# Transposing the blocks of a short convolution one pipeline tick later, with one input buffer turned into a working tile

## The chip, the core and the metric

The kernel runs on one core of a Trainium2 chip. The metric is device time in microseconds (us) of one execution, on a median of several runs. The core's engines work side by side, each through an instruction queue of its own: PE (TensorE, matrix products and transposes, with PEld for the loading of its stationary operand), DVE (VectorE), ACT (ScalarE), POOL (GpSimd) and SP (SyncE, which here issues the DMA transfers). [...]

## The reference, cut to what matters

The model is a two-layer backbone over 2048 latent tokens and 256 context tokens of width 1024. Layer 0 holds two groups of heads side by side, a gated DeltaNet with four heads of 128 (group A) and grouped-query attention (group B); layer 1 is a Conformer convolution. Every layer ends in an output projection and a gated residual. The change lies in the first step of group A. From the normalized, modulated input h and the weight w_in it computes 1536 channels (512 each of q, k and v), convolves each channel along the tokens with five taps, applies SiLU, and brings q and k of each head to unit length:

```python
def gdn_prep(qkv, a, b, conv_w, a_log, dt_bias):
    u = jax.nn.silu(depthwise_conv(qkv, conv_w))         # qkv = (h @ w_in)[:, :1536], 5 taps over tokens
    q, k, v = split_cols(u, [512, 512, 512])
    q = l2_normalize(heads(q, A_DK)) * (A_DK ** -0.5)    # a * rsqrt(sum(a * a) + NORM_EPS), per token and head
    k = l2_normalize(heads(k, A_DK))
    v = heads(v, A_DV)
    ...
```

The context tokens of k and v (not of q) go through the same step apart from the latent ones.

## The kernel before

All products are made of float32 values split into a high and a low part: `mm3` (L135 to L139) issues three matmuls for each slice of 128 of the contraction, high by high (L137), and the two cross terms (L138 and L139). With eight slices, one tile of products is 24 matmuls. `split` (L141) makes the two parts of a weight, the high one on ACT (L145), the low one mostly on POOL (L148).

Layer 0's input half runs as three stages: one that normalizes and transposes the tokens and projects the attention's values, then stage A (pool `stA`, L340 to L357), then stage B, which projects what is left. A long mixed stage follows (scan of the DeltaNet and attention), then the output projection and layer 1.

Stage A works in 56 blocks. A channel tile `ct` is one head of q (0 to 3), k (4 to 7) or v (8 to 11), and each has four blocks of 512 latent tokens; for k and v there is a fifth, of the 256 context tokens. `a_item` (L450) is the work of one block, cut in steps by `yield`:

- The 24 matmuls into a PSUM tile `ps_a` (pool `mm`, four tiles); the copy by ACT to the tile `ub` in SBUF (L459, five buffers); small copies by DVE that carry two tokens over from and to the neighbour block (L464, L465). With the second block of a channel tile the next tile's weights are loaded and split.
- An empty tick, then the taps: two multiplications by ACT into `acc` and `p1` (L474, L475), their sum by POOL (L476), three more taps by DVE (L478), and SiLU by ACT in place (L480). For q the result goes to memory here.
- One tick later the block is turned by PE with up to four transposes of 128 by 128 into `psT` (L488; pool `tp`, four PSUM tiles). For v, ACT copies it to `tok` (L492) and it is stored. For q and k, ACT squares it (L496), DVE sums the squares and scales them (L498, L500), and POOL raises to the power of -1/2 (L151). For q this is all; for k, DVE multiplies by the result into `tok` (L507) and it is stored.
- For k there is a further tick: four transposes back, `psB` (L513), a copy by ACT to `bt` (L515), and a store (L516).

`acc`, `p1`, `sq`, `bt` and a tile `ada_part` of another step share the tag `wk`, with five buffers in all. That step, `ada_late` (L1160), computes six pieces of the modulation of later stages: weights by DMA (L1170), multiply-adds by DVE (L1176, L1178), and small products by PE (`ps_adat`, L1183). It advances after the first and the fourth block of each channel tile.

Two things set the order on the engines. `pipe` starts one block per tick and then takes every block in flight one step on, newest first, so that the tick of a `yield` sets which block's matmuls are written ahead of which block's taps and transposes. What is written so is then ordered for each engine by a list scheduler, which takes the order of writing as the priority, holds an instruction back until it expects its operands and its buffer to be ready, and puts a later one in its place. A buffer of a tag comes from a pool of free ones, so that the number of buffers also takes part in the order. The order is fixed when the kernel is built; on the chip each engine follows its own.

Of the kernel before, what the change touches and what calls it, by code (L numbers as in the profile page):

```python
# [8 lines left out]
F32 = mybir.dt.float32  # L9
# [8 lines left out]
P = 128  # L18
# [90 lines left out]
class Build:  # L109
# [178 lines left out]
    def layer0_in(self):  # L288
        tc, nc = self.tc, self.nc
        with ExitStack() as es:  # L290
# [49 lines left out]
            with tc.tile_pool(name="stA", bufs=2, reuse_waits="tile") as st:  # L340
                self.ada1 = [self.kp.tile([P, 8], F32, name=f"ada1{x}") for x in "AB"]
                self.gcol = [self.kp.tile([P, 8], F32, name=f"gcol{x}") for x in range(2)]
                late = self.ada_late([(1, 2), (1, 0), (1, 3), (1, 1), (0, 4), (0, 5)],
                                     lambda: st.tile([P, 512], F32, tag="wk", name="ada_part", bufs=5))
                items = []
                cols = [ct * P for ct in range(12)]
                for ct in range(12):
                    blocks = [(0, 512), (1, 512), (2, 512), (3, 512)]
                    if ct >= 4:
                        blocks.append((4, TC))  # L350
                    shared = {}
                    for b, n in blocks:
                        items.append(self.a_item(ct, b, n, shared, st, cols[ct + 1] if ct < 11 else None))
                        if b in LATE_B:
                            items.append(late)
                self.pipe(items)
                self.pipe([late])  # L357
# [92 lines left out]
    def a_item(self, ct, b, n, shared, st, nxt):  # L450
        nc = self.nc
        kind, h = "qkv"[ct // 4], ct % 4
        whi, wlo = self.w0(ct * P, P)
        if b == 1 and nxt is not None:
            self.w0(nxt, P)
        ps = self.mm.tile([P, 512], F32, tag="mm", name="ps_a")
        self.mm3(ps[:, :n], [(whi[k], wlo[k], self.hhi[b][:, k, :], self.hlo[b][:, k, :]) for k in range(KT)])
        ub = st.tile([P, 516], F32, tag="ub", name="ub", bufs=5)
        nc.scalar.copy(ub[:, 2:2 + n], ps[:, :n])  # L459
        if b in (0, 4):  # L460
            nc.vector.memset(ub[:, 0:2], 0.0)
        else:
            prev = shared[b - 1]
            nc.vector.tensor_copy(ub[:, 0:2], prev[:, 512:514])  # L464
            nc.vector.tensor_copy(prev[:, 514:516], ub[:, 2:4])  # L465
        if b >= 3:
            nc.vector.memset(ub[:, 2 + n:4 + n], 0.0)
        shared[b] = ub
        yield
        yield  # L470
        w = [self.col("scw", ct * 5 + j) for j in range(5)]
        acc = st.tile([P, 512], F32, tag="wk", name="acc", bufs=5)
        p1 = st.tile([P, 512], F32, tag="wk", name="p1", bufs=5)
        nc.scalar.mul(acc[:, :n], ub[:, 0:n], w[0])  # L474
        nc.scalar.mul(p1[:, :n], ub[:, 1:1 + n], w[1])  # L475
        nc.gpsimd.tensor_tensor(out=acc[:, :n], in0=acc[:, :n], in1=p1[:, :n], op=ALU.add)  # L476
        for j in range(2, 5):
            nc.vector.scalar_tensor_tensor(out=acc[:, :n], in0=ub[:, j:j + n], scalar=w[j], in1=acc[:, :n],  # L478
                                           op0=ALU.mult, op1=ALU.add)
        nc.scalar.activation(acc[:, :n], acc[:, :n], AF.Silu)  # L480
        m = n // P
        tt0 = b * 4
        if kind == "q":
            nc.sync.dma_start(self.d_qT[h, :, tt0 * P:tt0 * P + n], acc[:, :n])
        yield
        psT = self.tp.tile([P, 4, P], F32, tag="tp", name="psT")
        for a in range(m):
            nc.tensor.transpose(psT[:, a, :], acc[:, a * P:(a + 1) * P], self.ident)  # L488
        if kind != "q":
            tok = st.tile([P, 4, P], F32, tag="tok", name="tok", bufs=3)  # L490
        if kind == "v":
            nc.scalar.copy(tok[:, :m, :], psT[:, :m, :])  # L492
            nc.sync.dma_start(self.d_v[tt0:tt0 + m, :, h * P:(h + 1) * P].rearrange("a p c -> p a c"), tok[:, :m, :])
            return
        sq = st.tile([P, 4, P], F32, tag="wk", name="sq", bufs=5)
        nc.scalar.activation(sq[:, :m, :], psT[:, :m, :], AF.Square)  # L496
        ss = st.tile([P, 4], F32, tag="ss", name="ssA")
        nc.vector.reduce_sum(ss[:, :m], sq[:, :m, :], axis=AX.X)  # L498
        f = 128.0 if kind == "q" else 1.0
        nc.vector.tensor_scalar(out=ss[:, :m], in0=ss[:, :m], scalar1=EPS, scalar2=f, op0=ALU.add, op1=ALU.mult)  # L500
        if kind == "q":

            self.rsqrt(self.rq[:, tt0:tt0 + m, h], ss[:, :m], m)
            return
        rn = st.tile([P, 4], F32, tag="rn", name="rn")
        self.rsqrt(rn[:, :m], ss[:, :m], m)
        nc.vector.tensor_tensor(out=tok[:, :m, :], in0=psT[:, :m, :],  # L507
                                in1=rn[:, :m].unsqueeze(2).to_broadcast([P, m, P]), op=ALU.mult)
        nc.sync.dma_start(self.d_k[tt0:tt0 + m, :, h * P:(h + 1) * P].rearrange("a p c -> p a c"), tok[:, :m, :])
        yield  # L510
        psB = self.tp.tile([P, 512], F32, tag="tp", name="psB")
        for a in range(m):
            nc.tensor.transpose(psB[:, a * P:(a + 1) * P], tok[:, a, :], self.ident)  # L513
        bt = st.tile([P, 512], F32, tag="wk", name="bt", bufs=5)
        nc.scalar.copy(bt[:, :n], psB[:, :n])  # L515
        nc.sync.dma_start(self.d_kT[h, :, tt0 * P:tt0 * P + n], bt[:, :n])  # L516

# [1029 lines left out]
```

## Time and profile before

| | |
|---|---|
| median of 3 runs | 2611.97 us (2608.75 to 2613.16) |
| profiled execution | 2612.17 us, span of its trace 2610.4 us, mean granted PE clock 0.99 |
| busy PE | 2518.3 us, 96% of the span |
| busy DVE, ACT, POOL | 1979.2 us (76%), 1466.5 us (56%), 1401.5 us (54%) |
| stage A on PE | from 112.28 us (first `ps_a`) to about 458 us (last `psT`) |
| memory traffic | 323.24 MB, mean 124 GB/s |

How to read it: the span is the time from the first to the last instruction of the trace, and lies 1.8 us below the time of the same execution. Busy times are sums over instructions; in a row of the timeline stand the start, the time, the engine, the line of the kernel and the operation with its output and inputs, and in brackets how long the engine sat idle before it and what ended that idle time. A row of the windows gives the busy time and the instructions of PE, PEld, DVE, ACT and POOL in a stretch, the granted PE clock as a share of full speed, the DMA share and GB/s. A row of the waits gives who waited for what, the total, the number of times and the longest.

### The profile page before, as it was taken

What the parts mean: (1) busy time and instruction counts of PE and PEld (TensorE: products, weight loads), DVE (VectorE), ACT (ScalarE), POOL (GpSimd) and SP (SyncE); (2) the same over time, 40 slices, a digit from 0 to 9 for tenths busy, and PEclk for the clock granted to TensorE, in tenths of its full rate; (3) what the DMA queues carried; (4) which work ended last, traced back from release to release, by engine and by line L of the source; (5) the groups of instructions that cost most, each with busy time, mean ns of one, the idle gap of its engine ahead of it and who ended that gap; (6) DMA issues with size and microseconds to landing.
All of it is one profiled execution on the core that took longest, in us unless ns stands there. A gap on an engine that the chain in (4) does not pass through costs nothing.

```text
span 2610.4 us, 43411 instructions
## 1 busy us (share of the span) xinstructions
PE 2518.3 (96%) x15072; PEld 2203.3 (84%) x15072; DVE 1979.2 (76%) x4118; ACT 1466.5 (56%) x3101; POOL 1401.5 (54%) x1189
## 2 busy tenths in 40 slices
PE   7999999999999799999999999999999999999998
PEld 5988878998888698999989998888888888888877
DVE  7566677676764787788777787746389999998875
ACT  7444456223776565656666666534266767666443
POOL 3344344566446473553354423012169999899775
PEclk9999999999999899999999999999999999999999
DMA  8133334334565755645564433134411211115643
GB/s 316 50 113 108 111 115 126 107 109 140 163 193 175 202 126 134 146 124 139 147 164 131 132 102 114 40 106 129 153 49 42 67 54 65 53 57 176 205 160 109
DMA packets 410747, 323.24 MB, mean 124 GB/s; under 512 B 131232, under 2 KB 339616, under 8 KB 410528
## 3 DMA queue, kind: packets, MB, share of 16 engines
q1 hardware_dynamic: 410528, 320.47, 41.1%
q8 instruction: 120, 1.97, 0.3%
q14 instruction: 99, 0.81, 0.1%
HBM read 216.05 MB, written 104.33 MB: 123 GB/s over the span
## 4 chain that ended last, share of the span: by engine, by line
PE 53%; DVE 7%; ACT 2%; issue 2%; DMA 2%; POOL 1%; SPq 0%; POOLq 0%; DVEq 0%; ACTq 0%
PE pt L1114 4%; PE ps_out L137 3%; PE ps_out L139 3%; PE ps_out L138 3%; PE pg L139 2%; PE pa L137 2%; PE pg L138 2%; PE pg L137 2%; PE pa L138 2%; PE pa L139 2%; PE pz L137 2%; PE pz L139 2%; PE pz L138 2%; PE po L1144 2%; PE po L1145 2%; PE po L1148 2%
## 5 line engine op out<-in xcount | busy, mean ns | idle before, releaser
L1406 DVE SCALAR_TENSOR_TENSOR pc<-u,hw,pc 128x1024 f32<-128x1024 f32 x320 | 390.0, 1281 | 5.2 <-ACT pc L1404 3.9
L1414 POOL TENSOR_TENSOR ac<-ac,pr 128x512 f32<-128x512 f32 x288 | 379.5, 1341 | 18.0 <-ACT pr L1413 4.4
L1413 ACT ACTIVATE pr<-u,hw 128x512 f32<-128x512 f32 x288 | 204.9, 721 | 91.3 <-POOL ac L1414 89.8
L1118 ACT CAST phi<-pt 128x512 fp32r<-128x512 f32 x288 | 164.5, 585 | 144.8 <-PE pt L1114 136.7
L137 PE MATMUL ps_b<-w_hi,hhi 128*128 128x256 f32 (+1 forms) x800 | 231.3, 291 | 8.8 <-DVE xn L572 6.8
L1119 DVE TENSOR_TENSOR plo<-pt,phi 128x512 fp32r<-128x512 f32 x288 | 195.6, 687 | 49.9 <-ACT phi L1118 46.7
L138 PE MATMUL ps_b<-w_lo,hhi 128*128 128x256 f32 (+1 forms) x800 | 227.6, 286 | 0.9 <-DVE w_lo L148 0.8
L139 PE MATMUL ps_b<-w_hi,hlo 128*128 128x256 f32 (+1 forms) x800 | 225.0, 287 | 0.6 <-POOL hlo L148 0.6
L1073 DVE TENSOR_SCALAR_CACHE_REDUCE S<-ps_s 128x512 f32<-128x512 f32 (+1 forms) x320 | 198.8, 631 | 16.1 <-PE ps_s L139 11.0
L1082 ACT ACTIVATE S<-S,m 128x1024 f32<-128x1024 f32 (+1 forms) x192 | 177.8, 929 | 49.0 <-DVE m L1079 48.5
L137 PE MATMUL ps_out<-wohi,yhi 128*128 128x512 f32 x512 | 201.9, 394 | 0.2 <-DVE x L1250 0.2
L139 PE MATMUL ps_out<-wohi,ylo 128*128 128x512 f32 x512 | 200.6, 393 | 1.4 <-DVE ylo L148 1.4
L138 PE MATMUL ps_out<-wolo,yhi 128*128 128x512 f32 x512 | 200.8, 392 | 0.0
L1144 PE MATMUL po<-phi,vhi 128*128 128x256 f32 x576 | 164.8, 306 | 14.4 <-ACT phi L1118 14.3
L1114 PE MATMUL pt<-ident,S 128*128 128x128 f32 x1152 | 175.3, 274 | 2.8 <-DVE plo L1119 1.9
L137 PE MATMUL ps_a<-hhi,w_hi 128*128 128x512 f32 (+1 forms) x448 | 172.1, 384 | 0.0
L138 PE MATMUL ps_a<-hlo,w_hi 128*128 128x512 f32 (+1 forms) x448 | 171.9, 384 | 0.0
L139 PE MATMUL ps_a<-hhi,w_lo 128*128 128x512 f32 (+1 forms) x448 | 171.3, 382 | 0.0
L478 DVE SCALAR_TENSOR_TENSOR acc<-ub,cols,acc 128x512 f32<-128x512 f32 (+1 forms) x168 | 136.4, 820 | 39.8 <-POOL acc L476 35.9
L137 PEld LDWEIGHTS ps_b<-w_hi,hhi 128*128 128x128 f32 x800 | 152.5, 191 | 12.2 <-issue 6.0
L138 PEld LDWEIGHTS ps_b<-w_lo,hhi 128*128 128x128 f32 x800 | 152.8, 191 | 2.3 <-DVE w_lo L148 1.8
L1145 PE MATMUL po<-phi,vlo 128*128 128x256 f32 x576 | 153.6, 286 | 0.0
(327 smaller groups left out, 7667.1 us busy)
## 6 DMA issues: line engine op xcount, KB each, us to landing
raw_ada<-in_ada_w_dram SPq DMA_DIRECT2D x48, 512.0 KB, 3.9
x<-in_x_dram SPq DMA_DIRECT2D x32, 512.0 KB, 10.3
kq<-d_kT SPq DMA_DIRECT2D x54, 256.0 KB, 3.1
raw_w<-in_ev_w_in_dram SPq DMA_DIRECT2D x26, 512.0 KB, 3.7
kq<-d_qT SPq DMA_DIRECT2D x48, 256.0 KB, 4.1
raw_w<-in_od_w_in_dram SPq DMA_DIRECT2D x24, 512.0 KB, 3.8
d_nt<-ntA SPq DMA_DIRECT2D x36, 256.0 KB, 4.3
vt<-d_v SPq DMA_DIRECT2D x36, 256.0 KB, 2.6
```

What stands on the lines that cost most here:

```text
L137: self.nc.tensor.matmul(ps, lhsT=lh, rhs=rh, start=(a == 0), stop=False)
L138: self.nc.tensor.matmul(ps, lhsT=lh, rhs=rl, start=False, stop=False)
L139: self.nc.tensor.matmul(ps, lhsT=ll, rhs=rh, start=False, stop=(a == n - 1))
L1073: nc.vector.tensor_scalar(out=S[g][:, k0:k0 + w], in0=ps[:, :w], scalar1=1.0, scalar2=None, op0=ALU.mult, op1=ALU.max, accum_out=mx[:, b:b ...
L1082: nc.scalar.activation(S[g], S[g], AF.Exp, bias=m, scale=scale, accum_out=l[:, g:g + 1])
L1114: nc.tensor.transpose(pt[:, e, a * P:(a + 1) * P], S[a][k0 // 1024][:, k0 % 1024:k0 % 1024 + P], self.ident)
L1119: nc.vector.tensor_tensor(out=lo, in0=pt, in1=hi.bitcast(F32), op=ALU.subtract)
L1144: nc.tensor.matmul(po, lhsT=vhi[:, ks], rhs=hi[:, e, :], start=(k == 0), stop=False)
L1145: nc.tensor.matmul(po, lhsT=vlo[:, ks], rhs=hi[:, e, :], start=False, stop=False)
L1406: nc.vector.scalar_tensor_tensor(out=pc, in0=s(j), scalar=w(j), in1=pc, op0=ALU.mult, op1=ALU.add)
L1413: nc.scalar.mul(pr, s(j), w(j))
L1414: nc.gpsimd.tensor_tensor(out=ac, in0=ac, in1=pr, op=ALU.add)
```

## The change

A second `yield` stands ahead of the transposes, so all that follows SiLU (the transposes, and for v the copy and store, for q and k the squares, sums and powers, for k the scaled tile, its store and the whole last step) is written one tick later than before. The tag `wk` gets six buffers where it had five, and `ub` four where it had five. The instructions and their operands are the same, and their number on every engine; from line 486 on, the changed kernel's lines count one more.

```diff
-                                     lambda: st.tile([P, 512], F32, tag="wk", name="ada_part", bufs=5))
+                                     lambda: st.tile([P, 512], F32, tag="wk", name="ada_part", bufs=6))
...
-        ub = st.tile([P, 516], F32, tag="ub", name="ub", bufs=5)
+        ub = st.tile([P, 516], F32, tag="ub", name="ub", bufs=4)
...
-        acc = st.tile([P, 512], F32, tag="wk", name="acc", bufs=5)
-        p1 = st.tile([P, 512], F32, tag="wk", name="p1", bufs=5)
+        acc = st.tile([P, 512], F32, tag="wk", name="acc", bufs=6)
+        p1 = st.tile([P, 512], F32, tag="wk", name="p1", bufs=6)
...
         yield
+        yield
         psT = self.tp.tile([P, 4, P], F32, tag="tp", name="psT")
...
-        sq = st.tile([P, 4, P], F32, tag="wk", name="sq", bufs=5)
+        sq = st.tile([P, 4, P], F32, tag="wk", name="sq", bufs=6)
...
-        bt = st.tile([P, 512], F32, tag="wk", name="bt", bufs=5)
+        bt = st.tile([P, 512], F32, tag="wk", name="bt", bufs=6)
```

The scheduler then lays the engines' orders anew. On PE, before, around the transposes of the block number 32 (counted from 0, a block of k): `ps_a_3712` is the product of block 40 and `ps_a_3758` that of block 41.

```order
L139 MATMUL ps_a_3712<-hhi4_115,w_lo_3208 128x256
L137 MATMUL ps_a_3712<-hhi4_115,w_hi_3207 128x256
L138 MATMUL ps_a_3712<-hlo4_116,w_hi_3207 128x256
L139 MATMUL ps_a_3712<-hhi4_115,w_lo_3208 128x256
L488 MATMUL psT_3433<-ident_62,acc_3361 128x128 x4
L137 MATMUL ps_a_3758<-hhi0_110,w_hi_3531 128x512
L138 MATMUL ps_a_3758<-hlo0_111,w_hi_3531 128x512
```

So before, nine products have been made, counting from block 32's own, when block 32 is turned. On PE, after the change, the transposes of the same block, where `ps_a_3512` is the product of block 37:

```order
L139 MATMUL ps_a_3512<-hhi1_412,w_lo_3185 128x512
L137 MATMUL ps_a_3512<-hhi1_412,w_hi_3184 128x512
L138 MATMUL ps_a_3512<-hlo1_413,w_hi_3184 128x512
L489 MATMUL psT_3470<-ident_62,acc_3340 128x128 x4
L139 MATMUL ps_a_3512<-hhi1_412,w_lo_3185 128x512
L137 MATMUL ps_a_3512<-hhi1_412,w_hi_3184 128x512
```

They have moved up, into the midst of block 37's product, behind five whole products and a third of a sixth. Counted over the whole stage, the products that lie ahead of a block's transposes number, before, four at the start, more and more from block 16 on up to nine at blocks 32 to 37, and four again from block 49; after, five to six at all blocks up to 51. At the last four blocks both orders have four, three, two and one.

On ACT, before, at the copies and multiplications of the k tiles (`ub_2921` is block 27's, and the copies to `ub` since then are those of `ub_2982`, `ub_3041`, `ub_3105` and `ub_3166`):

```order
L459 COPY ub_3166<-ps_a_3141 128x512
L515 COPY bt_3013<-psB_3008 128x512
L474 ACTIVATE acc_3046<-ub_2921,cols_60 128x512
L475 ACTIVATE p1_3047<-ub_2921,cols_60 128x512
L496 ACTIVATE sq_3061<-psT_3055 128x512
L515 COPY bt_3073<-psB_3070 128x256
L474 ACTIVATE acc_3109<-ub_2982,cols_60 128x512
```

A block's multiplications stand behind the copies of the four blocks after it. On ACT, after, at the same copy, block 31's, which is now `ub_3143` (`ub_3020` is block 29's):

```order
L459 COPY ub_3143<-ps_a_3118 128x512
L480 ACTIVATE acc_3088<-acc_3088 128x512
L516 COPY bt_3115<-psB_3112 128x256
L474 ACTIVATE acc_3146<-ub_3020,cols_60 128x512
L475 ACTIVATE p1_3147<-ub_3020,cols_60 128x512
L497 ACTIVATE sq_3161<-psT_3155 128x512
L145 CAST w_hi_3508<-raw_w_3506 128x1024
```

Here a block's multiplications stand behind the copies of one or two blocks after it. Beyond stage A the scheduler's times have moved too. In stage B the order is as before. In a part of the mixed stage, which follows at some 890 to 1260 us, it isn't; on ACT, before, around the copies of a DeltaNet state (`sbC`, L847 and L848) between the casts of the attention's turned scores (`phi`, L1118):

```order
L1118 CAST phi<-pt 128x512
L919 ACTIVATE W<-psw 64x2x64 x2
L1118 CAST phi<-pt 128x512
L847 ACTIVATE sbC<-sbT 64x1024
L848 ACTIVATE sbC<-sbT 64x1024
L1118 CAST phi<-pt 128x512 x4
```

On ACT, after, at the same place:

```order
L920 ACTIVATE W<-psw 64x2x64 x4
L1119 CAST phi<-pt 128x512
L848 ACTIVATE sbC<-sbT 64x1024
L1119 CAST phi<-pt 128x512
L849 ACTIVATE sbC<-sbT 64x1024
L1119 CAST phi<-pt 128x512 x3
```

One cast has moved between the two copies. On SP, two loads of `ada_late`'s weights stand earlier than before, and the stores of k and v one block later.

## Prediction

> **What bounds the kernel now.** I read the page first, then the windows by stage, then PE's waits in stage A, then its timeline around them, and last the two orders. The page's head:
>
> ```profile
> PE 2518.3 (96%) x15072; PEld 2203.3 (84%) x15072; DVE 1979.2 (76%) x4118; ACT 1466.5 (56%) x3101; POOL 1401.5 (54%) x1189
> ```
>
> PE is busy for 96% of the span, and no other engine comes near it. So a change that leaves the instructions alone can win only what PE waits, or what it loses to a lower clock. The windows: the q part of stage A, its k and v part, the start of stage B, and the part of the mixed stage whose order changes.
>
> ```profile
> 112.00:206.00 94.00, 94.00 (x442) 77.92 (x441) 55.41 (x108) 44.23 (x72) 42.56 (x29) 1.00 0.33 104
> 206.00:458.00 252.00, 242.83 (x1294) 205.45 (x1292) 177.03 (x323) 136.08 (x249) 102.19 (x76) 0.98 0.38 114
> 458.00:600.00 142.00, 137.44 (x1125) 135.35 (x1126) 106.08 (x383) 34.67 (x96) 87.63 (x117) 1.00 0.35 108
> 860.00:1200.00 340.00, 315.28 (x2314) 292.10 (x2315) 286.38 (x835) 208.43 (x538) 184.69 (x168) 0.95 0.57 141
> ```
>
> In the q part PE has no idle time and full clock: 16 blocks in 94.0 us are 5.9 us a block. In the k and v part it is idle for 252 − 242.8 = 9.2 us. DVE is at 70% there and POOL at 41%. PE's waits between 112 and 458 us name one cause:
>
> ```profile
> PE psT L488 <- ACT acc L480: 8.8, 8, 3.6
> PE psB L513 <- DVE tok L507: 0.2, 1, 0.2
> ```
>
> Nine microseconds in nine waits, and 8.8 of them are transposes that wait for SiLU. The largest, what comes after it, and the next largest:
>
> ```profile
> 379.33 0.28 PE L139 MATMUL ps_a<-hhi,w_lo 128*128 128x256 f32 x1
> 383.20 1.12 PE L488 MATMUL psT<-ident,acc 128*128 128x128 f32 x4 [3.59 <-ACT acc L480]
> 386.99 0.63 PE L137 MATMUL ps_a<-hhi,w_hi 128*128 128x512 f32 x1
> 389.25 0.40 PE L137 MATMUL ps_a<-hhi,w_hi 128*128 128x512 f32 x1
> 408.72 0.66 PE L488 MATMUL psT<-ident,acc 128*128 128x128 f32 x4 [0.81 <-ACT acc L480]
> 411.23 0.63 PE L138 MATMUL ps_a<-hlo,w_hi 128*128 128x512 f32 x1
> 446.26 0.66 PE L488 MATMUL psT<-ident,acc 128*128 128x128 f32 x4 [0.48 <-ACT acc L480]
> 455.23 0.66 PE L488 MATMUL psT<-ident,acc 128*128 128x128 f32 x4 [1.48 <-ACT acc L480]
> ```
>
> Both big waits are followed by matmuls of 0.63 us where 0.40 is usual. The windows around the two give the clock:
>
> ```profile
> 382.00:386.00 4.00, 2.80 (x8) 2.04 (x9) 3.08 (x3) 3.52 (x7) 3.31 (x2) 0.51 0.45 136
> 386.00:390.00 4.00, 4.00 (x13) 3.11 (x13) 3.93 (x6) 2.34 (x4) 2.14 (x3) 0.64 0.70 197
> 406.00:410.00 4.00, 3.06 (x21) 2.43 (x20) 2.03 (x6) 2.38 (x5) 0.31 (x1) 0.92 0.02 4
> 410.00:414.00 4.00, 4.00 (x13) 3.19 (x12) 2.23 (x8) 3.57 (x8) 1.71 (x2) 0.65 0.43 131
> ```
>
> Busy time times the missing clock is 2.80 × 0.49 + 4.00 × 0.36 = 2.8 us after the first, and 3.06 × 0.08 + 4.00 × 0.35 = 1.7 us after the second: 4.5 us. So stage A has 9.0 + 4.5 = 13.5 us to give.
>
> [...]
>
> **Why PE waits.** The transposes of one block stand in PE's order where the scheduler expected their input. This block's input passes through `ub`, ACT, POOL, DVE and ACT. Block 27's, on ACT: the copy into `ub`, the first multiplication, SiLU.
>
> ```profile
> 277.79 0.57 ACT L459 COPY ub<-ps_a 128x512 f32<-128x512 f32 x1
> 305.44 0.73 ACT L474 ACTIVATE acc<-ub,cols 128x512 f32<-128x512 f32 x1
> 313.96 0.63 ACT L480 ACTIVATE acc<-acc 128x512 f32<-128x512 f32 x1 [1.03 <-DVE acc L478]
> ```
>
> From multiplication to SiLU's end it takes 9.2 us. Ahead of that the block lies in `ub` for 27 us, since ACT's order puts its multiplication behind the copies of blocks 28 to 31 (the order rows above). PE runs nine products ahead. Nine is what the buffers hold, four PSUM tiles and five `ub`. When they are all taken, a late transpose leaves PE no product to do in the meantime, and the product behind it cannot start either: at 383 us ACT copies a PSUM tile free only as the 3.59 us gap ends.
>
> ```profile
> 383.06 0.57 ACT L459 COPY ub<-ps_a 128x512 f32<-128x512 f32 x1
> 383.97 0.78 PE L137 MATMUL ps_a<-hhi,w_hi 128*128 128x512 f32 x1
> ```
>
> **The change part by part.** *The second yield.* It adds no instruction. In the new order a block is turned some 5.3 products after its own began, through the whole k and v part. What must fit in between: its own product, the wait for its multiplication (one or two copies behind), and the 9.2 us to SiLU's end. Products first, in the k part:
>
> ```profile
> 239.22 0.60 PE L488 MATMUL psT<-ident,acc 128*128 128x128 f32 x4
> 369.28 0.38 PE L488 MATMUL psT<-ident,acc 128*128 128x128 f32 x2
> ```
>
> These are the transposes of blocks 16 and 35: 19 blocks in 130.1 us, 6.85 us a block, while PE was also building its lead of five products. A k channel tile has four blocks of 512 and one of half that, so of the 5.9 us of a q block (5.5 us product, 0.4 us transposes) remain 0.9 × 5.5 = 5.0 us, and two sets of transposes make it some 5.7 us. So 5.3 products are about 30 us; the block's own takes 5.7, its multiplication comes after one or two more, 5.7 to 11.4, and then 9.2: 20.6 to 26.3 us. That leaves 4 to 9 us of slack, and SiLU should be done when PE reaches the transposes. The waits of 9.0 us go, and the 4.5 us of clock with them. At the end of the stage both orders run out of products alike (four, three, two, one ahead), so the 0.48 and 1.48 us there stay: 13.5 − 2.0 = 11.5 us gained.
>
> What hangs on a moved block: the stores of k and v, the powers on POOL and the back transposes all come one tick later, and SP's queue with them. Their readers are in the mixed stage, over 400 us later, so this costs nothing. *`wk` with six buffers* pays for `acc`, which is now held a tick longer; with the old five the copy to `bt` or the next `acc` would wait. *`ub` with four buffers* lowers the greatest lead from nine to eight, which the new order, at five to six, doesn't use. Its price if it were short: a copy by ACT would wait for DVE's taps of the block four before. The block's multiplication is two products after its copy and the taps end 9.2 us on, so a buffer is free after about 11 + 9 = 20 us, and wanted after 4 × 5.7 = 23 us. That is the thinnest cover in this plan, 3 us.
>
> *The mixed stage.* Its order changes between some 890 and 1260 us as a by-product. The largest wait of PE there shows what such a shift is worth:
>
> ```profile
> 990.08 1.06 ACT L847 ACTIVATE sbC<-sbT 64x1024 f32<-64x1024 f32 x1 [5.75 <-DMA sbT<-d_nt]
> 995.29 0.58 PE L1144 MATMUL po<-phi,vhi 128*128 128x256 f32 x1 [5.41 <-ACT phi L1118]
> 995.00:1000.00 5.00, 4.71 (x22) 4.71 (x23) 4.72 (x12) 1.78 (x4) 2.09 (x2) 0.51 0.20 64
> ```
>
> ACT waits for a transfer ahead of casts that PE needs; PE is idle for 5.4 us and then loses 4.71 × 0.49 = 2.3 us, and with the slow rest before and after about 8.5 us in all (an estimate). The new order puts one cast between the two copies. That may take this stall away, leave it, or make another. I take 0 and keep ±8.5 us.
>
> **The sum.** The profiled execution took 2612.17 us, 0.2 us above the median: 2612.17 − 11.5 = 2600.7, so **2600.5 us**. Its own range: if the clock loss stayed without the waits, 2605; if the idle crumbs between matmuls go as well, 2595. So 2595 to 2606.
>
> **The rivals.**
>
> *The chain sets the pace (slower).* Before, PE could build a lead of nine products while transposes came every 6.85 us. In the new order the lead is fixed at 5.3, so if ACT, POOL and DVE need 6.85 us for a block however they are ordered, PE waits at each of the 19 blocks: 19 × (6.85 − 5.7) = 21.9 us, against the 13.5 us saved, and v blocks may add more. That is 2612.2 + 21.9 − 13.5 = 2620.5 us. It decides above 5.7 + 13.5/19 = 6.4 us a block. For it speaks that taps and the split of a weight get in each other's way, two taps taking 3.55 us beside a POOL subtraction where one alone takes 0.82:
>
> ```profile
> L478 DVE SCALAR_TENSOR_TENSOR acc<-ub,cols,acc 128x512 f32<-128x512 f32 (+1 forms) x168 | 136.4, 820 | 39.8 <-POOL acc L476 35.9 <-DMA d_k<-tok 1.9
> 313.18 3.55 DVE L478 SCALAR_TENSOR_TENSOR acc<-ub,cols,acc 128x512 f32<-128x512 f32 x2
> 313.68 2.50 POOL L148 TENSOR_TENSOR w_lo<-raw_w,w_hi 128x1024 fp32r<-128x1024 f32 x1
> ```
>
> [...] Against it: this comes once per channel tile and costs 1.9 us, DVE is only 70% busy, and of the 39.8 us that it sits idle ahead of its taps it waits 35.9 us for POOL's sum, which itself waits for ACT's late multiplication. Chance 0.10.
>
> *The gain is not kept.* The big gap had a second cause, the PSUM tile freed at 383 us; if copies to `ub` still come late with four buffers, or a transfer later in the kernel sets the time, little is left: 2611 us, 0.10. The chain of work that ended last speaks against it, since it runs on PE far more than on anything else:
>
> ```profile
> PE 53%; DVE 7%; ACT 2%; issue 2%; DMA 2%; POOL 1%; SPq 0%; POOLq 0%; DVEq 0%; ACTq 0%
> ```
>
> *The mixed stage gains too:* the 5.4 us stall goes, 2600.5 − 8.5 = 2592 us, 0.10. *It gains a second stall:* 2609 us, 0.08. A partial gain, some small waits in the k part, 2606 to 2609 us: 0.04.
>
> **How the numbers follow.** The forecast has 0.58. What a measurement can tell from no change is 0.2%, 5.2 us, so faster means below 2606.7 and slower above 2617.2. Faster: 0.58 + 0.10 + most of the partial case, 0.71. Same: 0.08 + 0.10 + the rest, 0.19. Slower: 0.10. The range reaches from 2590 to 2610: it leaves out the slower case, most of the unkept gain, and a tail of the doubled one.
>
> **What would show it.** In the new trace PE's waits for SiLU between 112 and 455 us fall to 2 or 3 us, no window there has a clock below 0.9, a block's copy and its multiplication lie 6 to 12 us apart instead of 27, and the last `psT` stands at about 446 us, with stage B as long as before. It is wrong if PE waits by a little at every block of k, evenly, which is the chain's pace; or if ACT waits ahead of copies to `ub` for DVE; or if stage A is 11 us shorter and the end isn't, which the length of the stretch from 860 to 1260 us would tell.

## The result and the profile after

| | before | changed |
|---|---|---|
| median | 2612.56 us (2608.75 to 2616.59, 6 runs) | 2597.53 us (2595.1 to 2599.97, 6 runs) |
| ratio | | 0.9945, 95% interval 0.9932 to 0.9958 |
| span of the first trace | 2610.4 us | 2598.2 us |

The changed kernel is faster by 15.0 us, where 11.5 us were forecast. One run of the kernel with four `wk` buffers (3100.4 us at a granted clock of 0.75) and one of the kernel before in the same series (3881.3 us at 0.60) were in a slow state and are left out. The page of the changed kernel's trace, its head:

```profile
span 2598.2 us, 43417 instructions
...
PE 2514.6 (97%) x15072; PEld 2199.8 (85%) x15072; DVE 1965.5 (76%) x4118; ACT 1466.6 (56%) x3101; POOL 1404.1 (54%) x1189
```

The windows of the changed kernel, the q part of stage A, its k and v part (which now ends before 446 us), and what follows:

```profile
112.00:206.00 94.00, 94.00 (x450) 78.27 (x450) 55.16 (x106) 45.55 (x75) 40.29 (x28) 1.00 0.32 101
206.00:446.00 240.00, 239.36 (x1307) 204.41 (x1305) 168.97 (x323) 136.66 (x251) 104.86 (x77) 1.00 0.40 121
446.00:600.00 154.00, 147.09 (x1204) 144.64 (x1203) 115.48 (x410) 37.35 (x102) 96.50 (x127) 1.00 0.37 116
```

PE is idle for 0.6 us of the 240 us where it was idle for 9.2 us, and its clock is full. What is left of its waits between 112 and 446 us:

```profile
PE psB L514 <- DVE tok L508: 0.3, 1, 0.3
PE psB L514 <- DVE ub L467: 0.3, 1, 0.3
```

No wait for SiLU is left. The first product of stage A and its last transposes, on PE after the change:

```profile
114.47 0.40 PE L137 MATMUL ps_a<-hhi,w_hi 128*128 128x512 f32 x1
...
444.96 0.38 PE L489 MATMUL psT<-ident,acc 128*128 128x128 f32 x2
```

Stage A takes 445.34 − 114.47 = 330.9 us, and took 457.99 − 112.28 = 345.7 us. These 14.8 us are about the whole gain of the medians. The spans of this pair of traces differ by 12.2 us only: the changed kernel's trace begins stage A 2.2 us later and takes 3.6 us more in the mixed stage, and its execution (2599.97 us) was the slowest of its six. The block whose way was shown before, number 27, goes through ACT like this now (copy, first multiplication, SiLU), and is turned by PE at 303.74 us:

```profile
277.65 0.59 ACT L459 COPY ub<-ps_a 128x512 f32<-128x512 f32 x1
...
290.86 0.72 ACT L474 ACTIVATE acc<-ub,cols 128x512 f32<-128x512 f32 x1
...
300.24 0.63 ACT L480 ACTIVATE acc<-acc 128x512 f32<-128x512 f32 x1 [0.71 <-DVE acc L478]
```

```profile
303.74 0.60 PE L489 MATMUL psT<-ident,acc 128*128 128x128 f32 x4
```

From multiplication to SiLU's end it takes 10.0 us, no less than the 9.2 us of before. What shrank is the time in `ub`, from 27.7 to 13.2 us, and SiLU now ends 2.9 us ahead of the transposes.

### The profile page after: what moved, and what is told of

Same layout as the page of the kernel before. It is cut to its first block, busy times and chain, and to the rows that moved or that the text cites. A ratio compares the mean times of both kernels' runs of the same rounds, so it can differ in the third digit from the quotient of the medians.

```text
span 2598.2 us, 43417 instructions
## 1 busy us (share of the span) xinstructions
PE 2514.6 (97%) x15072; PEld 2199.8 (85%) x15072; DVE 1965.5 (76%) x4118; ACT 1466.6 (56%) x3101; POOL 1404.1 (54%) x1189
## 4 chain that ended last, share of the span: by engine, by line
PE 53%; DVE 6%; ACT 3%; DMA 2%; issue 2%; POOL 1%; SPq 0%; POOLq 0%; DVEq 0%; ACTq 0%
PE pt L1115 4%; PE ps_out L137 3%; PE ps_out L139 3%; PE ps_out L138 3%; PE pz L137 2%; PE pz L139 2%; PE pg L139 2%; PE pz L138 2%; PE pa L137 2%; PE pg L138 2%; PE pg L137 2%; PE pa L138 2%; PE pa L139 2%; PE po L1145 2%; PE po L1146 2%; PE po L1149 2%
## 5 line engine op out<-in xcount | busy, mean ns | idle before, releaser
L1074 DVE TENSOR_SCALAR_CACHE_REDUCE S<-ps_s 128x512 f32<-128x512 f32 (+1 forms) x320 | 199.0, 630 | 19.4 <-PE ps_s L139 13.5
L1145 PE MATMUL po<-phi,vhi 128*128 128x256 f32 x576 | 163.7, 304 | 11.2 <-ACT phi L1119 10.9
```

What stands on the lines that cost most here:

```text
L1074: nc.vector.tensor_scalar(out=S[g][:, k0:k0 + w], in0=ps[:, :w], scalar1=1.0, scalar2=None, op0=ALU.mult, op1=ALU.max, accum_out=mx[:, b:b ...
L1145: nc.tensor.matmul(po, lhsT=vhi[:, ks], rhs=hi[:, e, :], start=(k == 0), stop=False)
```

## The experiments

The lead is the number of products that lie ahead of a block's transposes, counting from its own. The theory was that one tick between a block's taps and its transposes is what makes the lead grow: the scheduler finds the transposes' input not ready when they come up, puts later products there, ACT copies those ahead of the multiplications, and the next block is later still. What the scheduler expected was not read; that part is inferred from the orders. The rivals were that the buffers bring the gain, that it is the distance from product to transposes that counts, and that the chain through POOL and DVE sets the pace. In the diffs, `wk` and `ub` stand for the buffer counts of all tiles of the tag.

**The second yield alone** (against the kernel before):

```diff
+        yield
         psT = self.tp.tile([P, 4, P], F32, tag="tp", name="psT")
```

> The second yield alone, with the buffer counts of before (wk 5, ub 5). Theory (it is the tick between the taps and the transposes that decides, the buffers only pay for it): PE's order has five to six products ahead of a block's transposes here too, so PE's waits for SiLU in stage A stay under 2 us, no half clock there after 200 us, and the time is 2598 us, within 4 us. Rival (the sixth wk buffer is what lets it work): with five, the copies to bt or the next acc wait, PE waits for SiLU 5 us or more in stage A, and the time is 2605 us or more.

Measured: 2598.96 us, ratio 0.9955 (0.9942 to 0.9967). PE never waits for SiLU in stage A, and the stage takes 331.2 us. The gain is there without the buffers, within the intervals. What the sixth `wk` buffer does show in ACT's waits for a store of `bt` to free one, here three kinds:

```profile
ACT p L475 <- DMA d_kT<-bt: 6.4, 4, 2.9
ACT bt L516 <- DMA d_kT<-bt: 2.7, 2, 1.6
ACT sq L497 <- DMA d_kT<-bt: 0.9, 2, 0.5
```

and in the changed kernel one:

```profile
ACT acc L474 <- DMA d_kT<-bt: 3.2, 2, 2.5
```

They sum to 10.0 us, against 3.2 us, and cost PE nothing, but only just: at the v blocks 39 and 41 SiLU ends 0.2 and 0.1 us ahead of the transposes, where the changed kernel's least is 0.9 us.

**The buffers alone** (against before: `wk` 5 to 6, `ub` 5 to 4, one yield).

```diff
-    ... tag="wk", ... bufs=5       -    ... tag="ub", name="ub", bufs=5
+    ... tag="wk", ... bufs=6       +    ... tag="ub", name="ub", bufs=4
```

> The buffer counts alone (wk 6, ub 4), one yield ahead of the transposes as before. Theory: the lead of the products still grows through the k part, now up to eight, the wait for SiLU stays at 7 to 11 us and the time at 2612 us, within 5 us. Rival (the buffers bring the gain): waits under 4 us and 2605 us or less.

Measured: 2611.21 us, ratio 0.9999 (0.999 to 1.0008). The lead grows to its cap of eight, which is four PSUM tiles and four `ub`, and PE waits:

```profile
PE psT L488 <- ACT acc L480: 7.0, 4, 2.7
```

Stage A itself is 341.1 us long, 4.6 us shorter than before, yet the whole is not: from the first attention score to the output projection this kernel, whose order differs in the mixed stage too, takes 825.4 us in its trace, and the kernel before 820.0 us.

**Taps one tick earlier, transposes where they were** (against before):

```diff
         yield
-        yield
         w = [self.col("scw", ct * 5 + j) for j in range(5)]
...
         yield
+        yield
         psT = self.tp.tile([P, 4, P], F32, tag="tp", name="psT")
```

> Buffers as before (wk 5, ub 5); the empty tick ahead of the taps is taken out and put between the taps and the transposes, so the transposes are written at the tick of before and the taps one tick earlier. PE's order has 4.0 to 4.9 products ahead of a block's transposes. Theory (the distance from the taps to the transposes decides, two ticks are enough): PE waits for SiLU under 3 us in stage A, 2598 us, within 4 us. Rival (the distance from a block's product to its transposes decides, and four to five products are too few for copy, taps and SiLU): waits of 8 us or more spread over the k part, 2607 us or more.

Measured: 2599.91 us, ratio 0.9957 (0.9945 to 0.997). PE's waits between 112 and 460 us, without the 0.7 us in stage B:

```profile
PE psB L513 <- DVE tok L507: 1.7, 3, 0.9
PE psT L488 <- ACT bt L515: 0.8, 1, 0.8
...
PE psB L513 <- ACT ub L459: 0.5, 1, 0.5
PE psT L488 <- ACT acc L479: 0.2, 1, 0.2
```

So it isn't needed that blocks are turned later. With the lead at four to five, fewer products than before, two ticks from taps to transposes win nearly as much; stage A takes 334.1 us, the 3 us more being these waits.

**Both one tick earlier** (against before):

```diff
         yield
-        yield
         w = [self.col("scw", ct * 5 + j) for j in range(5)]
```

> Buffers as before; the empty tick ahead of the taps is taken out, and there is one tick between taps and transposes as before, so both are written one tick earlier. Theory: with one tick between them the lead starts at 3.2 and grows to 8.5 in the k part as before, and PE waits for SiLU 7 us or more in stage A: 2610 to 2618 us. Rival (the lead grows because the taps are written late): waits under 4 us, 2605 us or less.

Measured: 2616.97 us, ratio 1.0028 (1.0016 to 1.0041). The lead grows to 8.5 from a start of 3.4, PE waits 6.0 us for SiLU (the longest 3.2 us) and 3.3 us for a weight, and stage A takes 347.9 us. The wait for SiLU is 1 us short of what the theory expected, and the wait for a weight was in neither expectation. One tick between taps and transposes makes the drift, wherever the pair stands. This and the run before it tell the theory from the rival of distance.

**The second yield for the k blocks alone** (against the changed kernel):

```diff
         yield
-        yield
+        if kind == "k":
+            yield
         psT = self.tp.tile([P, 4, P], F32, tag="tp", name="psT")
...
         yield
-        yield
+        if kind == "k":
+            yield
         psT = self.tp.tile([P, 4, P], F32, tag="tp", name="psTb")
```

The second place is in `b_item`, stage B's step: there the transposes of all blocks but those of k lose a tick too, which the expectation does not name. What this run tells of stage A stands, but its whole time is that of two changes.

> The changed kernel with the second yield for the blocks of k alone; q and v have one, as before. In PE's order the lead in the k part is 5.0 to 5.5, in the q part it grows from four to six as before, and for v it is four. Theory (the loss comes from the k part's growing lead): no wait for SiLU in the k part, at most 2 us of such waits in all, and 2599 us within 4 us. Rival (q or v need the second tick as well): waits of 4 us or more outside the k part, 2604 us or more.

Measured: 2601.26 us, ratio 0.9957 (0.9945 to 0.997). One wait of 1.7 us for SiLU is left, at 381.7 us among the early v blocks, and 1.4 us for `tok`; stage A takes 333.5 us. The lead is 5.0 to 6.4 in the k part and 4.0 to 5.3 in the q part, as before the change. Of the 14.8 us by which the change shortens stage A, 12.2 come with the k blocks' yield. The stretch from stage A's end to the first attention score takes 411.7 us, so that stage B's lost tick shows no cost there.

**Three yields** (against the changed kernel, one more `yield` ahead of `psT`).

```diff
         yield
         yield
+        yield
         psT = self.tp.tile([P, 4, P], F32, tag="tp", name="psT")
```

> The changed kernel with a third yield ahead of the transposes, buffers as changed (wk 6, ub 4). The lead is six to seven. Theory (two ticks are already enough, PE has nothing left to wait for in stage A): stage A 331 us from the first product to the last transposes and 2598 us, within 4 us, no better than the changed kernel. Rival (acc, held for still longer, uses up the six wk buffers): ACT waits over 10 us for d_kT, PE waits for SiLU 2 us or more, 2602 us or more.

Measured: 2599.51 us, ratio 0.9949 (0.9934 to 0.9964); stage A 332.3 us, no wait for SiLU, and ACT waits 2.5 us in all for the store of `bt` (`d_kT`). Two ticks are enough, and the third brings nothing: stage A is 1.4 us longer, with a wait of PE of 1.4 us for an `ada_part`.

**Three `ub` buffers** (against the changed kernel, `ub` 4 to 3).

```diff
-        ub = st.tile([P, 516], F32, tag="ub", name="ub", bufs=4)
+        ub = st.tile([P, 516], F32, tag="ub", name="ub", bufs=3)
```

> The changed kernel with three ub buffers in place of four (wk 6). PE's order still has five to six products ahead. Theory (the fourth ub buffer has about 3 us to spare by the estimate, 0.6 us at the tightest block by the trace, so three are too few): copies to ub wait for DVE's taps in the k part, PE runs out of PSUM tiles there and waits 10 us or more in stage A, 2605 to 2620 us. Rival (four PSUM tiles behind the copies absorb it): PE waits under 3 us, 2598 us within 4 us.

Measured: 2602.57 us, ratio 0.9964 (0.9951 to 0.9977). Both expectations miss. PE waits 2.9 us for SiLU in two waits, the longer one here, and loses 1.7 us to half clock behind it (4.00 us busy at 0.57):

```profile
373.09 0.44 PE L489 MATMUL psT<-ident,acc 128*128 128x128 f32 x2 [2.31 <-ACT acc L480]
```

```profile
374.00:378.00 4.00, 4.00 (x12) 3.10 (x12) 2.81 (x7) 3.63 (x7) 1.36 (x2) 0.57 0.25 93
```

Stage A takes 335.7 us. Three buffers are too few by 5 us, not by 10 or more. The copies to `ub` do come late, those of blocks 30 to 32 begin 6.0, 5.0 and 7.7 us after their products end, where the changed kernel's begin after 0.4, 0.1 and 4.0 us; but no wait of PE is for a PSUM tile, so the four tiles take up this delay.

**Four `wk` buffers and two yields** (against before: the second yield, `wk` 5 to 4, `ub` 5).

```diff
-    ... tag="wk", ... bufs=5
+    ... tag="wk", ... bufs=4
...
+        yield
         psT = self.tp.tile([P, 4, P], F32, tag="tp", name="psT")
```

> The second yield with four wk buffers and five ub (the changed kernel has six and four). In this order the lead grows to six or seven in the k part. Theory (with five wk buffers ACT already waited 9 us for the store of bt to free one, with no wait on PE; with four those waits double and reach PE): ACT waits 15 us or more for d_kT, PE waits for SiLU 3 to 10 us in stage A, 2602 to 2612 us. Rival (wk does not matter while the two ticks are there): no wait on PE, 2598 us within 4 us.

Measured: 2614.70 us, ratio 1.0016 (1.0006 to 1.0025), worse than the theory's range. ACT waits 17.2 us for the store of `bt`, and PE 4.2 us for SiLU, the longest being this one:

```profile
ACT sq L497 <- DMA d_kT<-bt: 12.1, 9, 4.7
...
ACT acc L474 <- DMA d_kT<-bt: 5.1, 3, 3.1
```

```profile
385.13 0.47 PE L489 MATMUL psT<-ident,acc 128*128 128x128 f32 x1 [2.90 <-ACT acc L480]
```

The order has drifted as well (a lead of up to seven), and stage A takes 342.9 us, 11.7 us more than with five buffers. From its end to the first attention score it takes 416.2 us, 3.7 us more than with five; stage B begins in another order, but this stretch varies by as much between two traces of one kernel (below), so the cause of the rest stays open. So two ticks need five `wk` buffers, and four undo most of their gain in stage A and all of it in the whole.

**Both kernels a second time**, for what varies without any change.

> The kernel before once more, unchanged, for a second trace of it. If the stretches outside stage A differ between the first two traces by the change (theory: its new order in the mixed stage costs 3.5 us there), they come out here as in the first trace, within 1 us: the first product of stage A at 112.3 us, 820.0 us from the first attention score to the first product of the output projection. Rival (they vary from run to run): 2 us or more off in one of the two. In stage A the same waits for SiLU, 8 to 10 us, and half clock after the longest.

> The changed kernel once more, unchanged, for a second trace of it. Theory (the differences outside stage A are the change's): first product of stage A at 114.5 us, 823.6 us in the mixed stage, each within 1 us. Rival (they vary from run to run): 2 us or more off in one of them. In stage A no wait for SiLU and full clock either way, 331 us from the first product to the last transposes, within 1 us.

Measured: 2612.03 us and 2603.77 us, one run each. In the four traces, from PE's timeline (the lengths in us, "mixed" from the first attention score to the first product of the output projection):

| | before | before again | changed | changed again |
|---|---|---|---|---|
| first product of stage A | 112.3 | 112.6 | 114.5 | 112.7 |
| stage A | 345.7 | 345.0 | 330.9 | 330.4 |
| PE busy in stage A | 336.5 | 334.2 | 330.2 | 330.0 |
| end of stage A to first score | 414.7 | 415.9 | 412.0 | 415.3 |
| mixed | 820.0 | 817.4 | 823.6 | 825.2 |

Stage A repeats within 0.7 us. The late start in the changed kernel's first trace was that run's own. The mixed stage varies by 2.6 and 1.6 us between two traces of one kernel, so the theory that its 3.5 us are the new order's is not borne out: the second yield alone, three `ub` buffers, the earlier taps, three yields and the yield for k alone have the changed kernel's order in the mixed stage, and take 823.6, 827.8, 822.2, 820.2 and 828.0 us there. Nor is it refuted: none of the seven traces with the new order is below the two of before.

## Why the prediction was right, point by point

**PE's waits.** The prediction let 7.0 of the 9.0 us in stage A go, and all of them went. In its second trace the kernel before had more of them, so their size varies by a microsecond or two from run to run:

```profile
PE psT L488 <- ACT acc L480: 10.1, 10, 3.3
```

**The lost clock.** 4.5 us were counted. No window of the changed kernel's stage A is below full clock, so the loss is gone, but its size was one run's. In the second trace of before, the same two places:

```profile
382.00:386.00 4.00, 2.94 (x9) 2.03 (x10) 3.42 (x3) 2.98 (x7) 3.85 (x3) 0.62 0.46 137
386.00:390.00 4.00, 4.00 (x19) 3.23 (x18) 3.93 (x6) 2.34 (x4) 2.15 (x2) 0.96 0.73 200
406.00:410.00 4.00, 3.06 (x21) 2.80 (x22) 1.97 (x7) 2.07 (x5) 0.65 (x1) 1.00 0.07 21
410.00:414.00 4.00, 4.00 (x22) 3.39 (x22) 2.27 (x8) 3.87 (x8) 1.66 (x3) 1.00 0.37 115
```

That is 2.94 × 0.38 + 4.00 × 0.04 = 1.3 us, and nothing at 410 us. The slow stretch behind the 0.81 us wait, which the sum tied to that wait, did not come again.

**The tail, the term that was mis-sized.** 2.0 us of waits were kept since both orders run out of products of stage A alike. They went too. PE makes products of stage B between the last transposes, but their number is not what decides: before, 17, 31 and 15 of them stand ahead of the transposes of the last three blocks, after, 15, 35 and 11, and the kernel with the buffers alone has the 17, 31 and 15 of before and no wait there. What differs is where ACT casts stage B's first weight. Before, the cast waits for its transfer and the copy of block 52, whose product has ended at 430.81 us, stands behind it:

```profile
434.66 1.11 ACT L145 CAST w_hi<-raw_w 128x1088 fp32r<-128x1088 f32 x1 [2.47 <-DMA raw_w<-in_ev_w_in_dram]
435.67 0.58 ACT L459 COPY ub<-ps_a 128x512 f32<-128x512 f32 x1
```

After, the cast comes ahead of block 52's product, which runs from 414.97 to 420.71 us, and the copy follows 0.5 us behind that product's end:

```profile
413.13 1.11 ACT L145 CAST w_hi<-raw_w 128x1088 fp32r<-128x1088 f32 x1 [1.91 <-DMA raw_w<-in_ev_w_in_dram]
...
421.20 0.58 ACT L459 COPY ub<-ps_a 128x512 f32<-128x512 f32 x1
```

With the buffers alone the cast stands at 424.20 us, ahead of the end of that product at 428.62 us; with both one tick earlier it stands late, at 437.00 us, and the tail has a wait of 1.9 us. So in these traces the tail's waits go with the late cast; no run moves the cast alone.

**The sum, in part by luck.** With the 2.0 us the sum would have been 13.5; measured were 14.8 us in stage A in the first pair of traces and 14.6 us in the second. By the table above PE's idle time fell by 8.5 us in the first pair and by 10.4 in the second, and its busy time by 6.3 and 4.2. Of the busy time the lost clock is 4.5 and 1.3 us, so that 1.8 and 2.9 us of it are in no term of the sum; where they lie stays open. Waits and clock of the second trace of before add up to 10.7 + 1.3 = 12.0 us, against the 13.5 us of the first, so that the sum comes this near is in part the luck of the trace it was read from.

**The slack.** 4 to 9 us were worked out. For block 27 it is 2.9 us, over the k blocks 1.6 to 11.2 us, and at the early v blocks it falls to 0.9 us. A block's copy and its multiplication were to lie 6 to 12 us apart; over the k blocks it is 4.2 to 17.3 us. ACT at the tightest block, number 39, and PE:

```profile
368.67 0.73 ACT L474 ACTIVATE acc<-ub,cols 128x512 f32<-128x512 f32 x1 [2.51 <-DMA d_kT<-bt]
...
371.16 1.05 ACT L145 CAST w_hi<-raw_w 128x1024 fp32r<-128x1024 f32 x1 [0.69 <-DMA raw_w<-in_ev_w_in_dram]
...
373.83 0.92 ACT L480 ACTIVATE acc<-acc 128x512 f32<-128x512 f32 x2
```

```profile
375.39 0.60 PE L489 MATMUL psT<-ident,acc 128*128 128x128 f32 x4
```

SiLU, behind a wait for a `wk` buffer and one for a weight, ends about 1 us ahead of the transposes. The estimate had counted one block's chain and not what stands ahead of it in ACT's queue.

**The slower rival.** The chain does not set the pace: PE runs through the k part with no wait for SiLU, and makes its 20 blocks from 208.19 to 323.75 us, 5.8 us each, where 5.7 were estimated. Its sign was real all the same, two taps beside POOL's subtraction (2.85 us from 299.60 us) take as long as before, on DVE after the change:

```profile
299.47 3.54 DVE L478 SCALAR_TENSOR_TENSOR acc<-ub,cols,acc 128x512 f32<-128x512 f32 x2
```

The slack covers it. (The 0.82 us that the prediction sets against this is the mean of all taps, narrow and slowed ones too; the median of those of 128x512 is 0.75 us.)

**The buffers.** That `wk` needs the sixth buffer for the held `acc` was wrong: with five, the time is the same within the intervals, though the slack is nearly used up. That `ub` has few microseconds to spare was right, and three of them cost 5 us. Block 27's SiLU waits for DVE's taps until 300.24 us, which frees its `ub`; block 31's copy, the fourth after block 27's own, stands right behind:

```profile
300.77 0.57 ACT L459 COPY ub<-ps_a 128x512 f32<-128x512 f32 x1
```

**The mixed stage.** Taken at 0 with 8.5 us either way. The 5.4 us stall is gone in the changed kernel, where the longest of its kind is 2.6 us (3.0 us in its second trace), but other waits have come. PE's waits there, before (892 to 1285 us) and after (880 to 1270 us):

```profile
PE po L1144 <- ACT phi L1118: 6.5, 3, 5.4
PE pt L1114 <- DVE plo L1119: 1.6, 4, 0.9
PE ps_s L137 <- DVE S L1073: 0.8, 4, 0.2
```

```profile
PE po L1145 <- ACT phi L1119: 3.4, 2, 2.6
PE pt L1115 <- DVE plo L1120: 2.2, 4, 1.2
PE ps_s L137 <- DVE S L1074: 2.1, 3, 1.0
PE pt L1115 <- DVE sbT L856: 1.5, 1, 1.5
```

The sum of stage A's end to the output projection is 1234.7 and 1233.3 us in the traces of before, and 1232.3 to 1240.5 us in the seven with the new order of the mixed stage, 1237.1 us on the mean. Whether the new order costs a few microseconds there stays open; no kernel with the new stage A and the old mixed stage was run.

## What to carry to other kernels

When a list scheduler's order makes an engine wait, count, along that engine, how many products stand between a step's producer and its consumer, over the whole stage. Here a lead that grew from block to block until the buffers capped it was the sign of a consumer written before its input could be ready. Written as many ticks behind as the producer's chain lasts (9 to 10 us from multiplication to SiLU's end, against 5.8 us a tick, so two), the lead stays put; the number of buffers only set the cap at which the drift stopped, nine with five `ub` and eight with four. And read a stage's gain from that stage in two traces of the same kernel, since the other stages vary by 1 to 3 us between runs.

## What the runs showed of the hardware

Half clock doesn't follow from the length of a wait alone. In the run with the buffers alone two waits for SiLU are almost equal, at 329.85 and 386.54 us:

```profile
329.85 0.66 PE L488 MATMUL psT<-ident,acc 128*128 128x128 f32 x4 [2.70 <-ACT acc L480]
...
386.54 0.66 PE L488 MATMUL psT<-ident,acc 128*128 128x128 f32 x4 [2.66 <-ACT acc L480]
```

The stretches around the two waits, each 3.4 us wide to the nearest 0.1 us:

```profile
327.30:330.70 3.40, 0.66 (x4) 0.42 (x4) 2.66 (x6) 1.54 (x4) 1.94 (x2) 1.00 0.48 142
330.70:334.10 3.40, 3.31 (x10) 2.83 (x11) 2.09 (x7) 3.11 (x7) 1.45 (x2) 0.50 0.68 242
...
381.90:385.30 3.40, 1.99 (x17) 1.78 (x15) 3.40 (x3) 0.54 (x1) 3.38 (x3) 1.00 0.41 93
385.30:388.70 3.40, 2.16 (x11) 1.84 (x12) 3.40 (x7) 2.46 (x5) 0.00 (x0) 1.00 0.42 138
388.70:392.20 3.50, 3.50 (x17) 2.87 (x17) 3.50 (x7) 2.00 (x5) 1.92 (x1) 1.00 0.82 221
```

The first wait, from 327.15 to 329.85 us, lies almost wholly in one row and leaves PE busy for 0.66 of its 3.40 us; the next row runs at half clock, which costs 3.31 × 0.50 = 1.7 us. The second, from 383.88 to 386.54 us, is divided between two rows, which stay 1.99 and 2.16 us busy, and costs nothing.

The rows have this width since in the first traces of the two kernels the granted clock changes only at whole multiples of 3.41 us from one another. In stage A of the kernel before it is half for two such steps and for one; in the changed kernel's it never is. Rows of one step each, of the kernel before:

```profile
378.64:382.05 3.41, 0.97 (x9) 0.76 (x7) 3.38 (x6) 1.09 (x3) 1.28 (x1) 1.00 0.67 201
382.05:385.46 3.41, 2.26 (x7) 1.59 (x8) 2.48 (x3) 3.41 (x7) 2.77 (x2) 0.50 0.53 159
385.46:388.87 3.41, 3.41 (x9) 2.64 (x9) 3.34 (x5) 2.04 (x5) 1.98 (x2) 0.50 0.71 199
388.87:392.29 3.42, 3.42 (x19) 2.83 (x18) 3.42 (x7) 1.08 (x2) 1.42 (x1) 1.00 0.67 185
405.94:409.35 3.41, 2.47 (x19) 1.99 (x18) 2.09 (x6) 1.79 (x4) 0.00 (x0) 1.00 0.02 4
409.35:412.77 3.42, 3.42 (x10) 2.63 (x9) 1.96 (x7) 2.99 (x6) 1.09 (x2) 0.50 0.30 91
412.77:416.18 3.41, 3.41 (x20) 2.94 (x20) 2.41 (x2) 2.64 (x6) 2.51 (x2) 1.00 0.46 139
453.73:457.14 3.41, 1.93 (x17) 1.92 (x17) 2.31 (x6) 1.52 (x3) 0.23 (x1) 1.00 0.83 230
457.14:460.55 3.41, 3.41 (x30) 3.41 (x30) 0.83 (x4) 1.23 (x4) 0.00 (x0) 1.00 0.41 123
```

The 3.59 us wait, from 379.61 to 383.20 us, was divided between two steps too, and the clock fell within it, behind a step with PE busy for 0.97 us. The step with the 0.81 us wait had PE busy for 2.47 us, 0.95 us of them with eight products of a single column (`ps_adat`), and was followed by half clock; the one with the 1.48 us wait, at 453.73 us, had PE busy for 1.93 us only and was not. So in this trace neither the wait's length nor PE's busy time in the step tells which steps are followed by half clock, and what decides it is not shown. A wait's price in clock is thus a range, not a number: for the waits named here, in the first trace of before and in that of the buffers alone, it was 0 to 2.8 us.
